# First weight of the second mixer split among the last feed-forward products, in the places of its later values and keys; those products in a fixed order, the second block's projections in other banks

## The chip, the cores and the metric

The kernel runs on one core of a Trainium2 chip. The metric is the device time of one execution in microseconds (us), taken as the median of several executions of the same program. The engines are named as the profile names them: PE is TensorE (PEld its weight loads), DVE is VectorE, ACT is ScalarE, POOL is GpSimd, SP issues the DMAs.

## The reference

A trunk of two layers over 256 tokens of width 1024, in float32. Each layer has a mixer and a feed-forward part, each behind a modulation and ahead of a norm:

```python
for layer in range(DEPTH):
    shift, scale, gate = ada_modulation(c, ada_w[layer, 0], ada_b[layer, 0])
    h = x * (1.0 + scale) + shift
    y = mixer_ab(h, ...) if layer % 2 == 0 else mixer_c(h, ...)
    x = layer_norm(DN_ALPHA * x + gate * y, ln_g[layer, 0], ln_b[layer, 0])
    shift, scale, gate = ada_modulation(c, ada_w[layer, 1], ada_b[layer, 1])
    h = x * (1.0 + scale) + shift
    y = squared_relu_mlp(h, mlp_w1[layer], mlp_w2[layer])
    x = layer_norm(DN_ALPHA * x + gate * y, ln_g[layer, 1], ln_b[layer, 1])
```

The change lies at the seam between the feed-forward part of layer 0 and `mixer_c` of layer 1, which begins with `q, k, v = split(h @ w_in)` and a rotation (rope) of `q` and `k`.

## The kernel before

**Precision by parts.** Every float32 product is made of three: each operand is split into a high part (a cast on ACT, `wh`) and a low part (the difference, a subtraction on DVE, `wl`), and `mm3` adds high by high, high by low and low by high into one PSUM bank. `split` (L170) does the two steps and returns the low one.

**Weights.** `plan` lists every 1 MB weight block in the order in which it is wanted. `fill` issues their DMAs on SP into four raw buffers (`NRAW`), and issues the next one when a raw buffer has been split. `take` splits the next block in two halves, ("w1", l, i) and ("w2", l, i) for the feed-forward part, ("ci", j) for the second mixer's input projection. Halves go to the pool `sp`, six places for high parts and six for low parts (`NSPLIT`); a place is free again when the last product that reads it is done. `need(key)` takes blocks up to a key, `ahead(n)` takes the next n.

**Order.** The program is written in one order, but a scheduler makes each engine's queue from it: of the instructions that it believes ready it takes the one with the lowest priority number. An instruction's number is its place in the program; `later(n)` shifts it by n (table `LATER`, default 200 for splits), and `behind(what, m)` forces m to stand behind a remembered instruction on the same engine without a wait. Each engine then runs its queue strictly in that order.

**The seam.** `mlp(0, ...)` works through 16 blocks i of the hidden width: `first(i)` makes the hidden values (96 products with 256 columns, then relu, square and split: `r`, `uh`, `ul`), `second(i, b, h)` adds them into the outputs for token block b (0 or 1) and half h of the width (6 products with 512 columns). For layer 0 (`held`) the products of i = 13 for b = 1 and all of i = 14 and 15 are left for `finish(b)`: 60 products, the last ones of the layer. `finish` also adds the residual (`residual`, L611 to L613, three DVE steps for each half). `renew` (L641) then does, for b = 0 and for b = 1: `finish(b)`, `norm(b)` (DVE L617 and L619, the power on POOL at L305, DVE L629), `modulate` (eight PE transposes at L446, the affine step L451 on ACT and L454 on DVE, then the split into `hTh` and `hTl`). Around the norm of b = 0 it takes ci 0 and ci 1.

**The projection.** `c_project(0, ...)` (L1058) calls `products(part, b)` in the order (0,0), (1,0), (0,1), (1,1), (2,0), (2,1); part 0 is q, 1 is k, 2 is v. Each is 24 products over two blocks: part 0 needs ci 0 and 1, part 1 needs ci 2 and 3, part 2 needs ci 4 and 5. Within one, products 1 to 6 read the first half of the first block, 7 to 12 its second half, and so on. Each has a bank of the pair `a` (`pa`, two banks), which is read by the rope (L474 to L478 on DVE) or copied (v). The pair `d` (`pd`) holds the feed-forward outputs of b = 1 until their residual, and later the attention's outputs. `vv` has two places of 1040 columns (values of the two head groups, L1064), `keys` is the place of the second group's key block (L1061).

Of the kernel before, what the change touches and what calls it, by code (L numbers as in the profile page):

```python
# [45 lines left out]
LATER = {("ci", 0, 0): -1000, ("ci", 0, 1): -1000, ("co", 1, 1): -300, ("wo", 2, 0): 400, ("ada", 1, 5): 500, "cM1": 30, "cO011": -300, "cO100": 100, "wO010": 30, "wO110": -40, "wY10": -80}  # L46

BEHIND = {("ci", 0, 0): "moments", ("ci", 1, 0): "norm", ("ci", 1, 1): "norm"}
# [18 lines left out]
def trunk(ctx: ExitStack, tc, c, x, pos, small, ln, ada, w_g, w_g1, w_uq, w_out, c_in, c_out, w1, w2, out):  # L67
# [52 lines left out]
    def mlp_plan(l, more, room):  # L120

        more, p = list(more), [("w1", l, 0)]
        for i in range(16):
# [15 lines left out]
              "w1": lambda l, i: w1[l, i], "w2": lambda l, i: w2[l, i]}  # L139
    raw, parts, state = {}, {}, {"next": 0, "taken": 0, "half": 0, "critical": None, "rows": None, "copied": None, "columns": None}  # L140
# [29 lines left out]
    def split(dh, dl, src):  # L170

        nc.scalar.copy(dh, src)  # L172
        return nc.vector.tensor_sub(dl, src, dh.bitcast(F32))  # L173

    def take():
# [10 lines left out]
        elif key[0] == "ada":  # L186
            j = state["half"]
            with later(LATER.get(key, ADA_LATER)):
                state["half"] = ada_product(key, j, w[:, j * D:(j + 1) * D])
            if state["half"]:  # L190
                return
        else:
            cuts = (0, 1024, 2048)
            parts[key] = []
            for part, (lo, hi) in enumerate(zip(cuts, cuts[1:])):
                if key in (("w1", 0, 0), ("w1", 1, 0), ("w2", 0, 15)):
                    wh, wl = (work.tile([P, 1024], F32R, name=n, tag="q4", bufs=5) for n in ("wh", "wl"))
                elif key in (("wo", 0), ("co", 0)):
                    if lo == 0:
                        wide = [t.rearrange("p k q -> p (k q)") for t in new_hT()]  # L200
                    wh, wl = wide[0][:, lo:hi], wide[1][:, lo:hi]
                else:
                    wh = sp.tile([P, 1024], F32R, name="wh", tag="wh")[:, :hi - lo]
                    wl = sp.tile([P, 1024], F32R, name="wl", tag="wl")[:, :hi - lo]
                half = (*key, part)
                with later(LATER.get(half, SPLITS_LATER)):
                    state["split"] = split(wh, wl, w[:, lo:hi])
                    behind(BEHIND.get(half), state["split"])
                parts[key].append((wh, wl))
# [27 lines left out]
    def mm3(ps, a, b, start, stop):  # L237

        nc.tensor.matmul(ps, a[0], b[0], start=start, stop=False)  # L239
        nc.tensor.matmul(ps, a[0], b[1], start=False, stop=False)  # L240
        nc.tensor.matmul(ps, a[1], b[0], start=False, stop=stop)  # L241
# [381 lines left out]
    def norm(b, zst, between=lambda: None):  # L623
        z, st = zst
        mv, rs = moments(st)
        between()
# [14 lines left out]
    def renew(finish, gb, i):  # L641
# [4 lines left out]
        for b in range(NB):  # L646
            finish(b, zs[b])
            if b == 0:
                norm(b, zs[b], lambda: ahead(1))
                behind("norm", state["split"])  # L650
                ahead(1)
            else:
                norm(b, zs[b])
# [312 lines left out]
    def mlp(l, hT, rest, rows):  # L966
# [5 lines left out]
        def first(i):  # L972
# [10 lines left out]
            nc.scalar.activation(r, ps, AF.Relu)  # L983
# [24 lines left out]
        def second(i, b, h):  # L1008
            halves = need(("w2", l, i))
            for f in range(2):  # L1010
# [3 lines left out]
                mm3(acc[b][h], (us[i][0][:, s], us[i][1][:, s]), (wh[:, o], wl[:, o]),  # L1014
                    i == 0 and f == 0, i == 15 and f == 1)
# [7 lines left out]
        for i in range(16):  # L1023
            if i >= 1:
                need(("w2", l, i - 1))
            if i > 1:
                first(i)
            if i == at:
# [12 lines left out]
        def finish(b, zst):  # L1041
            if held and b:
                for h in range(2):
                    second(13, b, h)
            for h in range(2):
                for i in (14, 15):
# [11 lines left out]
    def c_project(g, got):  # L1058
# [10 lines left out]
        def products(part, b):  # L1069
            ps = pa("ps_c")  # L1070
# [111 lines left out]
```

## Time and profile before

| | us |
|---|---|
| median of 3 runs | 666.57 |
| lowest and highest | 666.43, 667.81 |
| the profiled execution | 669.87 |
| its span, first to last instruction | 668.0 |
| PE busy in it | 633.9 (95%) |

All rows come from the one profiled execution; times in them count from the start of its span. A PE row's duration is modelled and overlaps the next, so the pace is read from the starts. A row's last bracket is the idle time of the engine ahead of it, and what ended it.

### The profile page before, as it was taken

How to read it: one execution, taken by the hardware profiler on the slowest of the kernel's cores; microseconds unless marked ns; L12 is line 12 of the kernel's file. 1: busy time of each engine (PE TensorE's matmuls, PEld its weight loads, DVE VectorE, ACT ScalarE, POOL GpSimd, SP SyncE). 2: the span in 40 equal slices, each digit the busy share in tenths (PEclk: the TensorE clock that was granted, in tenths of full speed). 3: DMA queues.
4: the chain of work that ended last, by engine and by line, in shares of the span. 5: the costliest groups of instructions: out<-in, count | busy, mean ns of one | idle time of the engine just before them, and what ended most of it. 6: DMA issues, size and time to landing. Idle time of an engine off the chain costs nothing. (4 is left out here: it accounts for less than half of the span.)

```text
span 668.0 us, 9850 instructions
## 1 busy us (share of the span) xinstructions
PE 633.9 (95%) x3802; PEld 530.5 (79%) x3802; DVE 471.5 (71%) x887; ACT 339.2 (51%) x538; POOL 37.5 (6%) x69
## 2 busy tenths in 40 slices
PE   6998898989999999999988999999999999999994
PEld 3555676868898989898865888888899989898983
DVE  2859996257779989986796996755867755554447
ACT  3324676345545454545534555773654555545440
POOL 5010010100000000200020000000000100000004
PEclk9999998989999999999998999999999999999998
DMA  8993889033779997999642586411467765565101
GB/s 300 409 414 145 301 325 358 12 126 127 289 275 323 351 378 274 354 353 382 234 151 101 167 354 225 137 65 63 149 230 253 282 223 189 199 236 192 67 1 63
DMA packets 24385, 151.52 MB, mean 227 GB/s; under 512 B 2833, under 2 KB 3089, under 8 KB 8338
## 3 DMA queue, kind: packets, MB, share of 16 engines
q1 hardware_dynamic: 24194, 150.71, 61.1%
q8 instruction: 30, 0.49, 0.3%
q10 hardware_dynamic: 144, 0.18, 0.1%
q14 instruction: 17, 0.14, 0.1%
HBM read 149.83 MB, written 1.05 MB: 226 GB/s over the span
## 5 line engine op out<-in xcount | busy, mean ns | idle before, releaser
L172 ACT CAST wh<-w_w 128x1024 fp32r<-128x1024 f32 x128 | 131.0, 1051 | 150.7 <-PE ps_m L240 67.2
L173 DVE TENSOR_TENSOR wl<-w_w,wh 128x1024 fp32r<-128x1024 f32 x128 | 153.4, 1222 | 67.8 <-ACT wh L172 67.6
L239 PE MATMUL ps_m<-hTh,wh 128*128 128x256 f32 x448 | 126.7, 283 | 0.0
L241 PE MATMUL ps_m<-hTh,wl 128*128 128x256 f32 x448 | 126.6, 283 | 0.0
L240 PE MATMUL ps_m<-hTl,wh 128*128 128x256 f32 x448 | 126.6, 283 | 0.0
L241 PE MATMUL ps_m<-wh,ul 128*128 128x512 f32 x256 | 101.3, 396 | 0.4 <-DVE ul L173 0.4
L239 PE MATMUL ps_m<-wh,uh 128*128 128x512 f32 x256 | 101.1, 397 | 0.0
L240 PE MATMUL ps_m<-wl,uh 128*128 128x512 f32 x256 | 100.8, 395 | 0.0
L325 DVE CUSTOM_DVE_ANT_0 junk<-w_ada,cB,sm 128x1024 bf16<-128x1024 f32 x68 | 87.2, 1282 | 17.0 <-DMA w_ada<-in_ada_dram 15.6
L240 PEld LDWEIGHTS ps_m<-hTl,wh 128*128 128x128 f32 x448 | 85.7, 191 | 1.3
L239 PEld LDWEIGHTS ps_m<-hTh,wh 128*128 128x128 f32 x448 | 85.6, 191 | 1.2
L241 PEld LDWEIGHTS ps_m<-hTh,wl 128*128 128x128 f32 x448 | 85.7, 191 | 0.0
L241 PEld LDWEIGHTS ps_m<-wh,ul 128*128 128x128 f32 x256 | 48.2, 188 | 12.0 <-DVE ul L173 1.0
L239 PEld LDWEIGHTS ps_m<-wh,uh 128*128 128x128 f32 x256 | 48.3, 189 | 10.2 <-ACT uh L172 0.6
L240 PEld LDWEIGHTS ps_m<-wl,uh 128*128 128x128 f32 x256 | 48.2, 188 | 9.7 <-DVE wl L173 0.2
L239 PE MATMUL ps_c<-wh,hTh 128*128 128x512 f32 x96 | 38.7, 406 | 4.8 <-DVE rope L476 3.3
L240 PE MATMUL ps_c<-wl,hTh 128*128 128x512 f32 x96 | 38.7, 405 | 0.0
L241 PE MATMUL ps_c<-wh,hTl 128*128 128x512 f32 x96 | 38.0, 396 | 0.0
L173 DVE TENSOR_TENSOR ul<-relu,uh 128x512 fp32r<-128x512 f32 (+1 forms) x36 | 22.6, 627 | 17.6 <-ACT uh L172 17.6
L542 ACT ACTIVATE prob<-prob,negm 128x128 f32<-128x128 f32 (+1 forms) x64 | 26.8, 452 | 14.6 <-DVE negm L538 14.5
L173 DVE TENSOR_TENSOR wl<-w_ci,wh 128x1024 fp32r<-128x1024 f32 x24 | 28.7, 1218 | 7.0 <-ACT wh L172 6.9
L172 ACT CAST wh<-w_ci 128x1024 fp32r<-128x1024 f32 x24 | 24.9, 1050 | 13.2 <-PE ps_c L241 7.0
(231 smaller groups left out, 994.0 us busy)
## 6 DMA issues: line engine op xcount, KB each, us to landing
w_w<-in_w_dram SPq DMA_DIRECT2D x64, 1024.0 KB, 5.0
w_ada<-in_ada_dram SPq DMA_DIRECT2D x40, 1024.0 KB, 7.1
w_ci<-in_c_in_dram SPq DMA_DIRECT2D x12, 1024.0 KB, 5.9
w_ada<-in_ada_dram SPq DMA_DIRECT2D x12, 512.0 KB, 9.5
w_wo<-in_w_out_dram SPq DMA_DIRECT2D x4, 1024.0 KB, 4.8
w_co<-in_c_out_dram SPq DMA_DIRECT2D x4, 1024.0 KB, 5.1
w_g<-in_w_g_dram SPq DMA_DIRECT2D x8, 356.0 KB, 9.1
early<-in_ada_dram SPq DMA_DIRECT2D x4, 512.0 KB, 8.7
```

The lines of the kernel that those rows point to most:

```text
L172: nc.scalar.copy(dh, src)
L173: return nc.vector.tensor_sub(dl, src, dh.bitcast(F32))
L239: nc.tensor.matmul(ps, a[0], b[0], start=start, stop=False)
L240: nc.tensor.matmul(ps, a[0], b[1], start=False, stop=False)
L241: nc.tensor.matmul(ps, a[1], b[0], start=False, stop=stop)
L325: state[key, j] = nc.vector.tensor_tensor_reduce(out=junk, in0=w, in1=cB, scale=1.0, scalar=bias, op0=ALU.mult, op1=ALU.add, accum_out=m)
L542: state["exp"] = nc.scalar.activation(pr[:, j, :nk], pr[:, j, :nk], AF.Exp, bias=negm[:, hd:hd + 1], scale=-1.0)
```

## The change

It does seven things at the seam.

1. The blocks w2 15, ci 0 and ci 1 are taken at the top of i = 15, ahead of `first(15)`. Before, w2 15 was taken after `first(15)`, and ci 0 and ci 1 in `renew`, around the norm of b = 0.
2. The splits of w2 15 get the early number -300. The relu of `first(15)` must stand behind the second cast of w2 15 on ACT (`"early"`). The four casts of ci 0 and ci 1 must stand behind the cast `uh` of block 15, their four low parts behind `ul` of block 15.
3. The first half of ci 0 is split into the two places of `vv`; the second half into one place of `sp` (high) and the place of `keys` (low). Before, ci 0 held two high and two low places of `sp`.
4. The last low part of ci 1 must stand behind `moments` of b = 0 (L619). In `renew`, ci 2 is taken after the norm of b = 0 and ci 3 after that of b = 1, their low parts behind the norm just made.
5. The 60 last products have a fixed order (`"last"`): all of i = 14 for b = 0, i = 15 half 0, i = 15 half 1; then for b = 1 i = 13, i = 14, i = 15 half 0, i = 15 half 1.
6. The products (0,1), (1,1) and (2,1) of the first head group take a bank of the pair `d`.
7. `norm` loses its argument `between`; `split` also remembers the cast, `mm3` returns its three products.

```diff
-LATER = {("ci", 0, 0): -1000, ("ci", 0, 1): -1000, ("co", 1, 1): -300, ...}
-BEHIND = {("ci", 0, 0): "moments", ("ci", 1, 0): "norm", ("ci", 1, 1): "norm"}
+LATER = {("ci", 0, 0): -1000, ("ci", 0, 1): -1000, ("w2", 0, 15, 0): -300, ("w2", 0, 15, 1): -300, ("co", 1, 1): -300, ...}
+BEHIND = {("ci", j, part): "norm" for j in (2, 3) for part in range(2)}
...
+                elif key == ("ci", 0):
+                    if lo == 0:
+                        wh, wl = (work.tile([P, 1040], F32R, name=n, tag="vv", bufs=2)[:, :1024] for n in ("wh", "wl"))
+                    else:
+                        wh = sp.tile([P, 1024], F32R, name="wh", tag="wh")
+                        wl = work.tile([P, 6, 256], F32R, name="wl", tag="keys").rearrange("p a k -> p (a k)")[:, :1024]
...
+                if half == ("w2", 0, 15, 1):
+                    state["early"] = state["cast"]
+                if key in (("ci", 0), ("ci", 1)):
+                    firsts.append((state["cast"], state["split"]))
...
         for b in range(NB):
             finish(b, zs[b])
+            norm(b, zs[b])
             if b == 0:
-                norm(b, zs[b], lambda: ahead(1))
-                behind("norm", state["split"])
-                ahead(1)
-            else:
-                norm(b, zs[b])
+                behind("moments", firsts[-1][1])
+            ahead(1)
             modulate(zs[b][0], b, i, hT)
...
-            nc.scalar.activation(r, ps, AF.Relu)
+            m = nc.scalar.activation(r, ps, AF.Relu)
+            if held and i == 15:
+                behind("early", m)
...
+                for m in mm3(acc[b][h], (us[i][0][:, s], us[i][1][:, s]), (wh[:, o], wl[:, o]),
+                             i == 0 and f == 0, i == 15 and f == 1):
+                    if held and (i > 13 or b and i == 13):
+                        behind("last", m)
+                        state["last"] = m
...
+            if held and i == 15:
+                need(("w2", l, i))
+                ahead(2)
             if i > 1:
                 first(i)
+            if held and i == 15:
+                for cast, low in firsts:
+                    behind("cast", cast)
+                    behind("vector", low)
...
+            if held:
+                for h in range(2):
+                    second(14, b, h)
             for h in range(2):
-                for i in (14, 15):
+                for i in (15,) if held else (14, 15):
                     second(i, b, h)
...
-            ps = pa("ps_c")
+            ps = (pd if g == 0 and b else pa)("ps_c")
```

## Rows read from the trace of the kernel before

**Rows 1.** The page's first part, busy time of PE in the whole span.

```profile
PE 633.9 (95%) x3802; PEld 530.5 (79%) x3802; DVE 471.5 (71%) x887; ACT 339.2 (51%) x538; POOL 37.5 (6%) x69
```

**Rows 2.** Busy time of each engine in stretches of the seam. Columns: stretch, its length, then busy us and instructions of PE, PEld, DVE, ACT and POOL, the granted clock of PE, DMA share, GB/s.

```profile
339.19:340.64 1.45, 0.00 (x1) 0.00 (x1) 1.45 (x3) 1.45 (x3) 0.00 (x0) 1.00 0.79 311
...
348.37:349.56 1.19, 0.38 (x2) 0.00 (x0) 1.19 (x2) 0.00 (x0) 0.85 (x1) 1.00 1.02 420
...
350.97:354.69 3.72, 0.40 (x2) 0.03 (x1) 3.69 (x10) 1.93 (x5) 0.00 (x0) 1.00 0.34 139
354.69:358.27 3.58, 3.58 (x10) 2.75 (x11) 0.58 (x1) 0.59 (x1) 0.00 (x0) 0.52 0.00 0
358.27:384.00 25.73, 25.73 (x121) 20.83 (x120) 22.35 (x33) 14.51 (x17) 0.00 (x0) 1.00 0.46 146
```

**Rows 3.** Waits from 340 to 360 us: who waited for whom, us in total, times, longest.

```profile
PEld ps_c L239 <- issue: 3.7, 1, 3.7
...
PE ps_c L239 <- DVE rope L476: 3.3, 1, 3.3
```

**Rows 4.** Groups of PE's instructions from 340.6 to 354 us (products of the projection). Columns: line, engine, operation, out<-in, shapes, count, then busy us and mean ns of one, then idle time ahead of them by what ended it.

```profile
L239 PE MATMUL ps_c<-wh,hTh 128*128 128x512 f32 x12 | 4.9, 407 | 1.4 <-ACT hTh L172 1.4
L240 PE MATMUL ps_c<-wl,hTh 128*128 128x512 f32 x12 | 4.8, 403 | 0.0
L241 PE MATMUL ps_c<-wh,hTl 128*128 128x512 f32 x12 | 4.8, 397 | 0.0
```

**Rows 5.** Timeline of PE, from the first of the 60 last products to the first products of the projection. Columns: start, us, engine, line, operation, out<-in, shapes, count, idle time ahead.

```profile
323.55 0.39 PE L239 MATMUL ps_m<-wh,uh 128*128 128x512 f32 x1
...
336.27 1.08 PE L446 MATMUL ps_mod<-ident,z 128*128 128x128 f32 x8 [0.42 <-DVE z L629]
...
338.57 0.39 PE L240 MATMUL ps_m<-wl,uh 128*128 128x512 f32 x1
338.80 0.39 PE L241 MATMUL ps_m<-wh,ul 128*128 128x512 f32 x1
340.64 0.50 PE L239 MATMUL ps_c<-wh,hTh 128*128 128x512 f32 x1 [1.45 <-ACT hTh L172]
```

**Rows 6.** Timeline of PE's weight loads around the second block's transposes and the wait behind them.

```profile
349.56 0.87 PEld L446 LDWEIGHTS ps_mod<-ident,z 128*128 128x128 f32 x8 [1.23 <-DVE z L629]
350.40 0.19 PEld L239 LDWEIGHTS ps_c<-wh,hTh 128*128 128x128 f32 x1
...
354.66 0.26 PEld L239 LDWEIGHTS ps_c<-wh,hTh 128*128 128x128 f32 x1 [3.73 <-issue]
```

**Rows 7.** Timeline of DVE from the splits of w2 15 to the first rope.

```profile
325.98 1.23 DVE L173 TENSOR_TENSOR wl<-w_w,wh 128x1024 fp32r<-128x1024 f32 x1 [2.82 <-ACT wh L172]
327.12 0.68 DVE L173 TENSOR_TENSOR ul<-relu,uh 128x512 fp32r<-128x512 f32 x1
...
329.86 1.29 DVE L611 TENSOR_TENSOR z<-ps_m,gateB 128x512 f32<-128x512 f32 x2 [0.92 <-PE ps_m L241]
...
333.83 0.15 DVE L619 TENSOR_SCALAR rs<-mv 128x1 f32<-128x1 f32 x1
333.91 1.23 DVE L173 TENSOR_TENSOR wl<-w_ci,wh 128x1024 fp32r<-128x1024 f32 x1
335.57 1.00 DVE L629 TENSOR_SCALAR z<-z,mv,rs 128x512 f32<-128x512 f32 x2 [0.44 <-POOL rs L305]
...
346.54 0.14 DVE L619 TENSOR_SCALAR rs<-mv 128x1 f32<-128x1 f32 x1
...
348.25 1.70 DVE L629 TENSOR_SCALAR z<-z,mv,rs 128x512 f32<-128x512 f32 x2 [0.44 <-POOL rs L305]
...
354.13 0.42 DVE L476 TENSOR_TENSOR rope<-ps_c,sinT 128x256 f32<-128x256 f32 x1
```

**Rows 8.** Groups of DVE's instructions from 336.4 to 348.2 us, between the two norms; columns as in rows 4.

```profile
L173 DVE TENSOR_TENSOR wl<-w_ci,wh 128x1024 fp32r<-128x1024 f32 x5 | 6.0, 1203 | 0.0
```

**Rows 9.** Timeline of ACT at the seam.

```profile
323.75 0.60 ACT L983 ACTIVATE relu<-ps_m 128x512 f32<-128x512 f32 x1 [4.71 <-PE ps_m L241]
...
325.85 0.62 ACT L172 CAST uh<-relu 128x512 fp32r<-128x512 f32 x1
...
331.48 2.00 ACT L172 CAST wh<-w_ci 128x1024 fp32r<-128x1024 f32 x2 [2.17 <-PE ps_m L241]
...
339.00 1.07 ACT L172 CAST wh<-w_ci 128x1024 fp32r<-128x1024 f32 x1
339.94 1.17 ACT L172 CAST hTh<-h 128x512 fp32r<-128x512 f32 x2
...
351.79 1.14 ACT L172 CAST hTh<-h 128x512 fp32r<-128x512 f32 x2
```

**Rows 10.** DMA issues from 308 to 314 us: the blocks w2 14 and w2 15, count, KB each, median us from issue to landing.

```profile
w_w<-in_w_dram SPq DMA_DIRECT2D x2, 1024.0 KB, 5.4
```

**Rows 11.** Timeline of SP: the same two issues (from the start of the first to the end of the second).

```profile
309.84 2.75 SPq L166 DMA_DIRECT2D w_w<-in_w_dram  x2
```

**Rows 12.** Timeline of POOL: a fill of a key block long before the seam, a power alone, and the power and the fill at the second norm.

```profile
125.77 0.95 POOL L1063 MEMSET ckT__3690<- 64x1024 f32 x1
...
141.95 0.56 POOL L305 TENSOR_TENSOR rs<-rs,mhalf 128x1 f32<-128x1 f32 x1 [14.28 <-DVE rs L619]
...
346.76 1.46 POOL L305 TENSOR_TENSOR rs<-rs,mhalf 128x1 f32<-128x1 f32 x1 [11.22 <-DVE rs L619]
348.28 0.95 POOL L1063 MEMSET ckT__3689<- 64x1024 f32 x1
```

More of the change, by code (lines that the diff above doesn't have):

```diff
@@ L45 @@
 SPLITS_LATER, ADA_LATER, ROWS_LATER = 200, 300, 0
-LATER = {("ci", 0, 0): -1000, ("ci", 0, 1): -1000, ("co", 1, 1): -300, ("wo", 2, 0): 400, ("ada", 1, 5): 500, "cM1": 30, "cO011": -300, "cO100": 100, "wO010": 30, "wO110": -40, "wY10": -80}
-BEHIND = {("ci", 0, 0): "moments", ("ci", 1, 0): "norm", ("ci", 1, 1): "norm"}
+LATER = {("ci", 0, 0): -1000, ("ci", 0, 1): -1000, ("w2", 0, 15, 0): -300, ("w2", 0, 15, 1): -300, ("co", 1, 1): -300, ("wo", 2, 0): 400, ("ada", 1, 5): 500, "cM1": 30, "cO011": -300, "cO100": 100, "wO010": 30, "wO110": -40, "wY10": -80}
+BEHIND = {("ci", j, part): "norm" for j in (2, 3) for part in range(2)}
 X_STEPS = ({8: 4, 9: 4}, 13), ({i: 1 for i in range(3, 11)}, 12)
@@ L139, in trunk @@
               "w1": lambda l, i: w1[l, i], "w2": lambda l, i: w2[l, i]}
+    firsts = []
     raw, parts, state = {}, {}, {"next": 0, "taken": 0, "half": 0, "critical": None, "rows": None, "copied": None, "columns": None}
@@ L170, in split @@
     def split(dh, dl, src):
-        nc.scalar.copy(dh, src)
+        state["cast"] = nc.scalar.copy(dh, src)
         return nc.vector.tensor_sub(dl, src, dh.bitcast(F32))
@@ L237, in mm3 @@
     def mm3(ps, a, b, start, stop):
-        nc.tensor.matmul(ps, a[0], b[0], start=start, stop=False)
-        nc.tensor.matmul(ps, a[0], b[1], start=False, stop=False)
-        nc.tensor.matmul(ps, a[1], b[0], start=False, stop=stop)
+        return [nc.tensor.matmul(ps, a[0], b[0], start=start, stop=False),
+                nc.tensor.matmul(ps, a[0], b[1], start=False, stop=False),
+                nc.tensor.matmul(ps, a[1], b[0], start=False, stop=stop)]
     crow = work.tile([1, 1040], F32, name="crow", tag="vv", bufs=2)[:, :D]
@@ L621, in moments, with norm @@
         return mv, rs
-    def norm(b, zst, between=lambda: None):
+    def norm(b, zst):
         z, st = zst
         mv, rs = moments(st)
-        between()
         for h in range(2):
@@ L1013, in second @@
                 o = slice(h * 512, (h + 1) * 512)
-                mm3(acc[b][h], (us[i][0][:, s], us[i][1][:, s]), (wh[:, o], wl[:, o]),
-                    i == 0 and f == 0, i == 15 and f == 1)
+                for m in mm3(acc[b][h], (us[i][0][:, s], us[i][1][:, s]), (wh[:, o], wl[:, o]),
[3 more added lines that the diff above has]
+                        state["last"] = m
         need(("w1", l, 1))
```

## The prediction

> **What bounds the kernel now.** I read the page's busy shares first: PE works 633.9 of 668.0 us [rows 1], so nothing but PE's idle time, and time at a low clock, can be won. The table of stretches then says where at this seam: PE stands still or nearly so in 339.19 to 340.64, 348.37 to 349.56 and 350.97 to 354.69, and in the 3.58 us behind the last of these it is busy at a mean granted clock of 0.52, that is mostly at the lower of its two levels, 1.2 GHz [rows 2]. Third, the waits and timelines name what each waited for. The pace of dense work is 0.23 us from one product of 512 columns to the next (338.57 to 338.80), and 0.105 us for a transpose (eight in 0.84 us, 349.56 to 350.40) [rows 5, 6]. Against that pace the seam loses:
>
> - before the first block's transposes, 0.42 us for the norm [rows 5];
> - before the first projection product, from 338.80 to 340.64, 1.84 - 0.23 = 1.61, for `hTh` [rows 5];
> - before the second block's transposes, 1.19 - 0.23 = 0.96, for the second norm [rows 2, 6];
> - before product block (0,1), 3.72 - 0.23 = 3.49 [rows 2]. The weight load is labelled "issue" with 3.7, but the product itself waits for DVE's L476 [rows 3], the last reader of (0,0)'s bank, which starts at 354.13 [rows 7];
> - at the low clock, 3.58 for six products and four transposes, worth 6 x 0.23 + 4 x 0.105 = 1.80, so 1.78 [rows 2].
>
> Together 8.26 us. That is the ceiling of the change, give or take half a microsecond of short waits.
>
> Why PE runs dry at 350.97 is in the groups: 3 x 12 = 36 projection products were done [rows 4], block (0,0) with 24 and half of (1,0) with 12. By the code the six places hold ci 0, 1 and 2; ci 3 needs a place of ci 0, which (0,1) must read first, and (0,1) needs a third bank where pair `a` has two. The input was there earlier: `hTh` of b = 1 is cast from 351.79, its first half being done some 0.6 later, at 352.4 [rows 9].
>
> **The change part by part.** *Banks.* (0,1) takes a bank of pair `d`, whose reader is the residual of b = 1, finished before the second norm at 348.25 [rows 7]. The wait for L476 goes. What is late next is `hTh` at 352.4: alone, the banks save 354.69 - 352.4 = 2.3 us, and PE's standstill shrinks to 1.4. Standstills of 1.2 and 1.45 left the clock at 1.00 in the next stretch, the one of 3.72 did not [rows 2], so I count the 1.78 too: 4.1 us.
>
> *Places.* ci 0 now holds one high and no low place of `sp`, so ci 1, ci 2 and the first half of ci 3 fit beside it (high 1 + 2 + 2 + 1, low 2 + 2 + 1). (1,0) can run 18 products ahead of (0,1) instead of 12: 6 x 0.23 = 1.4 us more cover. The last quarter needs a cast and a low part (1.07 + 1.23 [rows 7, 9]) while (0,1) has 12 products (2.8 us) left: hidden; uncovered it would cost 2.3.
>
> *Splits moved forward.* Between the two norms DVE makes five low parts of ci, 6.0 us [rows 8], in front of or within the chain that makes the second norm. With ci 0 done before the first norm, at most three are left there (ci 2, perhaps one of ci 1; ci 3 must follow the second norm). So the second norm comes 2 x 1.2 = 2.4 us earlier, and up to 3.6. Where do the moved ones go? ACT idles 4.71 ahead of the relu of block 15 and DVE 2.82 ahead of w2 15's first low part [rows 7, 9]. w2 15 is issued about 312.3 and lands 5.4 later, near 317.7 [rows 10, 11], so its two casts (2.0) fit before 323.75 and its low parts (2.4) into the 2.82. Then `uh`, now at 325.85 behind one of those casts, and `ul` come some 0.8 earlier, and ci 0's low parts fill 326.5 to 329, where DVE now works on w2 15 and waits 0.92 [rows 7]. The relu now waits for w2 15 on ACT; queued behind are `uh` and the casts of ci, and PE needs `uh` at 323.55 + 12 x 0.23 = 326.3. A landing 2 us late would still be covered.
>
> *Fixed order.* The 60 products take 13.8 us either way. Half 0 of b = 0 is complete after 18, near 327.9, half 1 after 24, near 329.3; now both residuals begin at 329.86 [rows 7]. DVE, with ci 0's low parts ahead, begins near 329.0 and needs the same 4.1 us for six steps and the moments. So the first norm moves by 0 to 1 us earlier, or 0.3 later if a low part of ci 1 gets in front; I take 0.6, the start of the residual moved from 329.86 less a little. A further low part still stands beside the power, as now (333.91). Behind the norm, the cast of ci at 339.00 now stands in front of `hTh` [rows 9]; the changed places let the casts of ci 1 and 2 go earlier, but their slots still come free with i = 13 and 14 of b = 1, near 332 and 335. I estimate that of the 2.03 us lost at the first norm and `hTh`, 1.0 is won (bounds -0.3 and 2.0).
>
> *Second norm.* With 1.0 from the start and 2.4 from the low parts, `hTh` of b = 1 is there between 349.0 and 350.0. PE starts the projection at 339.64 and has 42 products and eight transposes: 9.66 + 0.84 leads to 350.1. The standstill closes. So all of 0.96 + 3.49 + 1.78 = 6.23 goes; I leave 0.5 for imperfect order.
>
> *Key and value places.* The value blocks and the second key block can be filled only when ci 0 has been read, near 350. The fill of 0.95 that now runs at 125.77 [rows 12] then lands in a busy stretch of DVE. The price by rows: the second norm's pair took 1.70 where the first took 1.00 [rows 7], beside a fill of 0.95 [rows 12]: 0 if no such step is beside it, 0.7 if one is. It isn't needed until the second group's keys, four blocks of 24 products or 22 us on; I take 0, since few of DVE's steps there are of the norm's kind. The power shows the same kind of contact: 0.56 alone, 1.46 beside a low part [rows 12].
> The Trainium skill (SBUF — State Buffer, Who interferes with whom) speaks against this move: DVE and GpSimd share a port pair under an exclusive lock, held for a whole instruction, and the loser blocks entirely. By that rule the fill could cost its full 0.95, and the sum would give 661.5; the trace agrees in kind, with 0.70 for a fill of 0.95.
>
> *DVE behind the seam.* From 350.97 to 384.00 DVE is busy 3.69 + 0.58 + 22.35 = 26.6 of 33.0 us [rows 2]: 6.4 idle. PE's work there moves some 6 us forward. DVE's low parts and ropes must follow, and not every gap can be used. It was relieved of two low parts; I book 0.7 given back (bounds 0 and 4).
>
> **Sum.** 1.0 + 6.23 - 0.5 - 0.7 = 6.0 us. The profiled execution of 669.87 would become 663.9; it lies 3.3 above the median, so I take the difference off the median: 666.57 - 6.0 = **660.6**. After 384 PE is dense, so what is won at the seam should stay won.
>
> **The rivals.**
> *Banks alone.* The scheduler leaves low parts in front of the second norm, so `hTh` stays at 352.4. For it: those low parts have no idle time ahead of them [rows 8]. Against: two low parts are forced forward by the order. 4.1 saved: 662.4.
> *DVE takes it back.* The seam gains as above, but ropes and low parts fall behind by up to the 4 us of the bound above: 664.6. For it: 6.4 us of idle time against 6 needed. Against: eight steps of the new x in that stretch can wait.
> *The fill meets the chain.* The fill that moves to 350 stands beside a step of DVE on which PE waits, and costs the 0.70 of the second norm: 661.3. For it: DVE is busy then. Against: the wait must also reach PE.
> *It doesn't do what it says.* The first norm moves later and the ahead-of-need splits meet slots that come free no earlier; the bank's gain is eaten: 666 to 667.
> *Slower.* A standstill like the one at 350.97 comes back twice in the projection, because DVE's strict queue has a low part that waits for a place in front of a rope. Each costs 3.49 + 1.78 = 5.27, so two give 660.6 + 10.5 = 671. It decides from the second on: one alone leaves 665.9.
>
> **Chances.** Forecast, with its own range 658.5 to 662: 0.50; the fill 0.10; banks alone 0.16; DVE takes back 0.09; nothing 0.07; slower 0.08. Times within 0.2% (1.3 us) can't be told from no change by this measurement; so faster 0.85, same 0.07, slower 0.08. The range goes from the ceiling, 666.57 - 8.26 - 0.5 = 657.8, to just past the second rival, 664.8; it leaves out "nothing" and "slower".
>
> **What would show it.** Right: no wait of `ps_c` for L476; 42 products before (0,1), no granted clock under 1.00 near 350; two fewer low parts of ci between the norms; the second norm near 345; `uh` of block 15 near 325; (0,1) starting near 350. Wrong: PE waiting for `wl` of w2 15 or ci 3; the first norm later than 335.6; casts of ci in front of L451 on ACT; DVE without a gap and PE waiting for ropes from 350 to 376.

## The result and the profile after

| | before | after |
|---|---|---|
| median, us (4 runs each, on one chip) | 667.19 | 660.59 |
| lowest and highest | 666.43, 671.20 | 659.38, 662.98 |
| the profiled execution, and its span | 669.87, 668.0 | 662.98, 661.1 |
| first of the 60 last products to the first attention product (`ps_s`), in the trace | 59.57 | 53.33 |

The ratio is 0.9893, with a 95% interval of 0.9844 to 0.9942: faster, by 6.6 us, where 6.0 was forecast. In the traces 6.24 us of it lie between the first of the 60 last products (323.55 before, 323.29 after) and the first attention product (383.12 and 376.62). From there to the end both run nearly equally long, 284.84 and 284.49 us. Below, "the seam" is the stretch from the first of the 60 to that attention product.

The page's first part, of after, which answers to [rows 1]: span less PE's busy time is 661.1 - 631.9 = 29.2 us, where it was 34.1.

```profile
PE 631.9 (96%) x3802; PEld 530.6 (80%) x3802; DVE 470.5 (71%) x887; ACT 339.1 (51%) x538; POOL 34.4 (5%) x69
```

The stretches of the seam after, in the columns of [rows 2]:

```profile
323.29:335.36 12.07, 12.07 (x55) 9.82 (x54) 11.07 (x16) 8.18 (x10) 1.06 (x1) 1.00 0.78 297
337.79:340.28 2.49, 0.39 (x2) 0.00 (x0) 2.16 (x6) 2.41 (x6) 0.00 (x0) 1.00 0.49 204
340.28:346.19 5.91, 5.80 (x24) 4.42 (x25) 5.17 (x10) 0.00 (x0) 0.55 (x1) 1.00 0.19 43
346.19:349.60 3.41, 3.41 (x19) 2.94 (x20) 3.34 (x7) 2.68 (x6) 0.00 (x0) 1.00 0.56 238
349.60:352.40 2.80, 2.80 (x14) 2.29 (x13) 2.73 (x6) 0.06 (x1) 0.00 (x0) 1.00 0.00 0
352.40:376.62 24.22, 24.22 (x115) 19.54 (x113) 20.37 (x29) 14.43 (x17) 2.16 (x4) 1.00 0.49 169
```

Only one stretch is left in which PE stands still, 337.79 to 340.28; from there on PE is busy for all but 0.11 us, and the granted clock is 1.00 throughout, where the stretch behind the rope wait had 0.52 [rows 2]. The view of PE's waits from 323 to 377 us has one line; the rope's 3.3 [rows 3] and two waits for the norms are gone. The wait that is left, for the first `hTh`, has grown from 1.4 [rows 4] to 2.1:

```profile
PE ps_c L250 <- ACT hTh L173: 2.1, 1, 2.1
```

PE's timeline after, in the columns of [rows 5]:

```profile
336.22 1.03 PE L457 MATMUL ps_mod<-ident,z 128*128 128x128 f32 x8
337.01 0.48 PE L252 MATMUL ps_m<-wh,ul 128*128 128x512 f32 x1
337.32 0.39 PE L250 MATMUL ps_m<-wh,uh 128*128 128x512 f32 x1
337.55 0.40 PE L251 MATMUL ps_m<-wl,uh 128*128 128x512 f32 x1
337.79 0.39 PE L252 MATMUL ps_m<-wh,ul 128*128 128x512 f32 x1
340.28 0.51 PE L250 MATMUL ps_c<-wh,hTh 128*128 128x512 f32 x1 [2.10 <-ACT hTh L173]
...
346.19 1.11 PE L457 MATMUL ps_mod<-ident,z 128*128 128x128 f32 x8
...
351.26 0.40 PE L250 MATMUL ps_c<-wh,hTh 128*128 128x512 f32 x1
```

The first transposes no longer wait: 56 of the 60 products stand ahead of them and four behind, where it was 52 and eight. The same four products are then missing as cover for `hTh`, and the standstill ahead of the first projection product is longer than before, 2.49 us from start to start (337.79 to 340.28) where it was 1.84. The row at 351.26 is the first product of block (0,1), 42 projection products having run ahead of it; it waits for nothing.

DVE's timeline after, which answers to [rows 7]:

```profile
325.44 0.69 DVE L174 TENSOR_TENSOR ul<-relu,uh 128x512 fp32r<-128x512 f32 x1 [0.27 <-ACT uh L173]
326.39 2.36 DVE L174 TENSOR_TENSOR wl<-w_ci,wh 128x1024 fp32r<-128x1024 f32 x2 [0.26 <-ACT wh L173]
328.67 1.28 DVE L622 TENSOR_TENSOR z<-ps_m,gateB 128x512 f32<-128x512 f32 x2
...
332.26 1.21 DVE L174 TENSOR_TENSOR wl<-w_ci,wh 128x1024 fp32r<-128x1024 f32 x1
333.39 0.20 DVE L628 BATCH_NORM_AGGREGATE mv<-stats 128x2 f32<-128x12 f32 x1
333.63 0.15 DVE L630 TENSOR_SCALAR rs<-mv 128x1 f32<-128x1 f32 x1
333.70 1.22 DVE L174 TENSOR_TENSOR wl<-w_ci,wh 128x1024 fp32r<-128x1024 f32 x1
335.36 1.00 DVE L639 TENSOR_SCALAR z<-z,mv,rs 128x512 f32<-128x512 f32 x2 [0.44 <-POOL rs L316]
...
336.88 1.21 DVE L174 TENSOR_TENSOR wl<-w_ci,wh 128x1024 fp32r<-128x1024 f32 x1
338.01 0.72 DVE L465 TENSOR_SCALAR h<-ps_mod,facA,facB 128x128 f32<-128x128 f32 x2
...
345.59 1.00 DVE L639 TENSOR_SCALAR z<-z,mv,rs 128x512 f32<-128x512 f32 x2 [0.67 <-POOL rs L316]
```

The residual begins 1.19 us earlier (0.93 counted from the start of the seam), but the first norm does not: 12.07 us from that start, 12.02 before. A low part of ci 1 (332.26) stands between the residual's last step and the moments. The second norm comes 2.66 us earlier, at 345.59 [rows 7]. Between the two norms two low parts of ci are left, at 336.88 and 342.67, of five [rows 8].

ACT and POOL after, which answer to [rows 9] and [rows 12]:

```profile
324.79 0.62 ACT L173 CAST uh<-relu 128x512 fp32r<-128x512 f32 x1
...
336.86 2.21 ACT L462 ACTIVATE h<-ps_mod,facB,facA 128x128 f32<-128x128 f32 x6 [0.96 <-PE ps_mod L457]
339.09 1.14 ACT L173 CAST hTh<-h 128x512 fp32r<-128x512 f32 x2
...
348.42 1.24 ACT L173 CAST hTh<-h 128x512 fp32r<-128x512 f32 x2
```

```profile
334.26 1.06 POOL L316 TENSOR_TENSOR rs<-rs,mhalf 128x1 f32<-128x1 f32 x1 [53.80 <-DVE rs L630]
...
345.00 0.55 POOL L316 TENSOR_TENSOR rs<-rs,mhalf 128x1 f32<-128x1 f32 x1 [9.68 <-DVE rs L630]
...
353.14 0.95 POOL L1086 MEMSET ckT__3689<- 64x1024 f32 x1
354.48 0.95 POOL L1086 MEMSET ckT__3690<- 64x1024 f32 x1 [0.39 <-PE ps_c L251]
```

`hTh` of b = 1 is done 348.42 + 1.24 = 349.66, 1.6 us before (0,1) wants it at 351.26. The fills have moved behind the last read of ci 0, to 353 and 354. That of the second group's keys must, by the change's step 3; the other one, which stood beside the second norm at 348.28 [rows 12], stands behind the fills of `vv` in POOL's queue. With it gone the second norm's pair takes 1.00 us (345.59), where it took 1.70 [rows 7].

### The profile page after: what moved, and what is told of

It is laid out like the page before. It is cut to its first block, busy times and chain, and to the rows that moved or that the text cites. A ratio compares the mean times of both kernels' runs of the same rounds, so it can differ in the third digit from the quotient of the medians.

```text
span 661.1 us, 9849 instructions
## 1 busy us (share of the span) xinstructions
PE 631.9 (96%) x3802; PEld 530.6 (80%) x3802; DVE 470.5 (71%) x887; ACT 339.1 (51%) x538; POOL 34.4 (5%) x69
## 3 DMA queue, kind: packets, MB, share of 16 engines
HBM read 149.83 MB, written 1.05 MB: 228 GB/s over the span
```

## The experiments

Each kernel was timed beside the kernel before, in three groups, each on one chip. The medians of one and the same program lie up to 2.7 us apart between the groups (before: 666.54, 667.99, 669.19), so the seam's length, read from one trace of each, is the finer measure: in the thirteen traces the seam begins anywhere from 319.34 to 324.05 us, and what follows it takes 284.4 to 284.8. "Lost" is the seam less 50.28 us, which is what its 204 products and 32 transposes take at the pace (0.23 and 0.105 us [rows 5, 6]). "Clock" is the mean granted clock of the seam.

| kernel | median, runs | ratio to before, 95% | seam, us | lost, us | clock |
|---|---|---|---|---|---|
| before | | | 59.57 | 9.29 | 0.97 |
| the change (first result) | 660.59, 4 | 0.9893 [0.9844, 0.9942] | 53.33 | 3.05 | 1.00 |
| banks_alone | 664.31, 12 | 0.9944 [0.9913, 0.9974] | 55.69 | 5.41 | 1.00 |
| places_banks | 663.17, 8 | 0.9913 [0.9879, 0.9947] | 53.81 | 3.53 | 1.00 |
| no_banks | 663.79, 12 | 0.9950 [0.9924, 0.9976] | 56.51 | 6.23 | 0.97 |
| no_places | 662.21, 6 | 0.9902 [0.9866, 0.9938] | 54.50 | 4.22 | 0.97 |
| whole_change | 661.96, 8 | 0.9914 [0.9883, 0.9946] | 54.39 | 4.11 | 0.97 |
| free_order | 664.35, 12 | 0.9950 [0.9921, 0.9979] | 55.47 | 5.19 | 0.97 |
| low_parts_split | 662.73, 8 | 0.9910 [0.9876, 0.9943] | 52.35 | 2.07 | 1.00 |
| low_parts_behind | 660.57, 6 | 0.9889 [0.9851, 0.9928] | 52.51 | 2.23 | 1.00 |
| w2_unforced | 662.23, 7 | 0.9901 [0.9867, 0.9936] | 55.33 | 5.05 | 1.00 |
| low_part_behind_hTl | 659.61, 6 | 0.9867 [0.9824, 0.9909] | 52.40 | 2.12 | 1.00 |
| whole_change_again | 661.47, 6 | 0.9892 [0.9855, 0.9928] | 54.49 | 4.21 | 0.97 |

My theory was the sum of the prediction: most of the gain is the third bank and the low clock behind its wait, the rest comes from low parts that leave the two norm chains. The rival for the second half was that the banks alone do it, and that the rest of the change is idle.

**banks_alone.** The kernel before, with this line of the change only:

```diff
-            ps = pa("ps_c")
+            ps = (pd if g == 0 and b else pa)("ps_c")
```

> The kernel before with one edit: the projections of b = 1 in the first head group take banks of pair d. Theory (each part of the change takes its own share): the wait for the rope's L476 goes, (0,1) starts when hTh of b = 1 is cast, near 352.4, PE stands still 1.4 us instead of 3.7, the granted clock stays at 1.00: 2.3 + 1.8 = 4.1 us faster than before, ratio 0.994. Rival A (the banks are the whole change): 6.5 us faster, ratio 0.990. Rival B (the standstill is long enough for the low clock all the same): 2.3 us, ratio 0.9965.

The seam lost 59.57 - 55.69 = 3.88 us of its length, where 4.1 was priced. The product of (0,1) in its timeline:

```profile
350.07 0.50 PE L239 MATMUL ps_c<-wh,hTh 128*128 128x512 f32 x1 [1.10 <-ACT hTh L172]
```

The wait for L476 is gone, `hTh` is next with a standstill of 1.50 start to start (1.4 priced), and no low clock follows. So in the traces the bank is the larger half of the change, and not all of it. The medians allow 3.9 us, but they can't tell this kernel from the whole change: the intervals of the two ratios overlap.

**places_banks.** The same, and the places of ci 0 as in step 3 of the change:

```diff
+                elif key == ("ci", 0):
+                    if lo == 0:
+                        wh, wl = (work.tile([P, 1040], F32R, name=n, tag="vv", bufs=2)[:, :1024] for n in ("wh", "wl"))
+                    else:
+                        wh = sp.tile([P, 1024], F32R, name="wh", tag="wh")
+                        wl = work.tile([P, 6, 256], F32R, name="wl", tag="keys")...
```

> The kernel before with the banks of d and the places of ci 0, but with the splits taken and ordered as before. Theory: 42 products are ready ahead of (0,1) instead of 36, but the low part of ci 3 comes only behind the second norm, near 351.3, so PE works on from there: about 1.1 us more than the banks alone, 5.2 us faster than before, ratio 0.992; the second norm stays near 348. Rival A (banks are all): the same as the banks alone. Rival (the places matter most): as the whole change, 6.5.

The seam is 53.81 us: 1.88 less than with the banks alone, and only 0.48 more than with the whole change. (0,1) now has 42 products ahead of it and starts at 350.13, behind no standstill. The second norm starts where it did before (24.72 us from the start of the seam, 24.70 before). Six products more ahead of (0,1) are 1.4 us of cover; the other half a microsecond has another source. The fill no longer stands beside the second norm, whose pair took 1.70 us with the banks alone (first row) and takes 1.00 here (second row):

```profile
345.86 1.70 DVE L629 TENSOR_SCALAR z<-z,mv,rs 128x512 f32<-128x512 f32 x2 [0.44 <-POOL rs L305]
```

```profile
346.50 1.00 DVE L635 TENSOR_SCALAR z<-z,mv,rs 128x512 f32<-128x512 f32 x2 [0.44 <-POOL rs L311]
```

So the first half of `hTh` is cast by 28.17 us into the seam and not by 28.88 (the start of the casts and 0.62), and (0,1) starts at 28.35 and not at 28.93. The wait for the second transposes shrinks from 0.94 to 0.25 for the same reason.

The four steps that this kernel lacks (the order in which the splits are taken and forced, and that of the last products) together add the last 0.48 of the 6.24 us. Its median ratio, 0.9913, can't be told from those of the whole change, 0.9893, 0.9914 and 0.9892. Its standstill ahead of the first projection product is still 1.83 us, where the change's is 2.49, and two of the three traces of the change have a low clock behind that (below) and with it a longer seam, 54.39 and 54.49, than this kernel's.

**no_banks.** The change without its line on the banks:

```diff
-            ps = (pd if g == 0 and b else pa)("ps_c")
+            ps = pa("ps_c")
```

> The whole change without its banks: all projections in pair a. Theory: with the splits moved forward the rope of (0,0) is read by 351.6 in the changed kernel, while PE is busy with 42 products until about 351.1, so the bank comes free at almost the moment it is wanted: 0.3 to 1.0 us slower than the whole change, still 5.5 to 6.2 us faster than before, ratio 0.991. Rival A (the banks are the whole change): 4 us or more of the gain are lost, ratio 0.996 or above, and the low clock is back.

Its waits of PE in the seam:

```profile
PE ps_c L250 <- ACT hTh L173: 2.1, 1, 2.1
PE ps_c L250 <- DVE rope L487: 1.5, 2, 1.1
```

The rope waits are back, and two, as the rival "slower" had it; but one at a time they cost 0.56 and 1.23 us, not 3.49 each, and no low clock follows them. I had expected 0.3 to 1.0 for this kernel; the two waits alone are 1.8. Most of what is left of the 56.51 - 53.33 = 3.2 is a low clock further ahead, behind the standstill before the first projection product; against the two traces of the change that have one too, the seam is 2.0 to 2.1 longer.

**no_places.** The change without the six lines of places_banks, so that ci 0 goes to the pool `sp` as before (the diff there, taken back).

> The whole change, but ci 0 is split into pool sp as before. Theory: 36 products lead to about 349.8 and hTh of b = 1 is cast from 348.4 on, so (0,1) needs no more cover: 0 to 0.5 us slower than the whole change, ratio to before 0.990 to 0.991. Rival (the places make the gain, by cover and by early splits): 1.4 us or more slower than the whole change, ratio 0.992 or above, PE standing still ahead of (0,1).

54.50 us, but with a low clock in it that the first trace of the change did not have; against the two traces of the change that have one (54.39 and 54.49, below) it is 0.0 to 0.1 longer. (0,1) comes after 36 products, at 27.79 us, 0.3 behind the end of `hTh`. Without the low clock, about 1.1 us, it would meet `hTh` and wait for some of that; here too the fill is back beside the second norm, whose pair takes 1.71. So by this estimate the places are worth between 0 and 0.8 us once the splits are moved forward, and 1.88 where they are not: two remedies for one wait.

**whole_change and whole_change_again.** The changed kernel, without an edit, in the second and the third group, as measure of the kernels beside it.

> The changed kernel itself once more, beside the three below. It should give 0.989 of the kernel before, with an interval of about 0.4% to either side, and in its trace some 53.3 us from the first of the last 60 feed-forward products to the first attention product, the standstill of 2.5 us before the first value product in it again, since the order of the queues makes it. What is open is the low clock: behind the same standstill the trace of the changed kernel had none, and two of the experiments had a stretch of granted clock near 0.6. If it comes by chance from one execution to the next, this trace may have it, and is then some 1.7 us longer (55 us); if it hangs on the places and banks, it has none.

> The changed kernel beside the two others of this call, as their measure. It should lie 1.5 to 2.5 us above the kernel with the low part behind hTl and 0.5 to 1.5 us below the one with w2 15 unforced. In its trace the standstill of 2.49 us stands again before the first query product; of its two traces so far one had a low clock behind it (seam 54.39 us) and one had none (53.33 us), so either may come.

(In these texts and in those of low_parts_split and low_parts_behind, "value product" and "value weight" are slips: the first projection product is that of q, block (0,0), and the weight meant is ci 1, the second one of q.) Up to the first projection product both traces are the first one to within 0.02 us: norm at 12.06 and 12.07, that product at 16.99 and 16.99. Behind it both have the low clock. Of the latter, the standstill and what follows:

```profile
337.04:339.53 2.49, 0.39 (x2) 0.00 (x0) 2.16 (x6) 2.41 (x6) 0.00 (x0) 1.00 0.51 214
339.53:343.00 3.47, 3.46 (x9) 2.75 (x10) 3.47 (x5) 0.00 (x0) 0.00 (x0) 0.55 0.02 5
```

Nine products in 3.47 us at a mean granted clock of 0.55, that is mostly 1.2 GHz; in the first trace 15 ran in the 3.47 us behind the same standstill. Six products are 1.4 us; 0.26 of it comes back, since the second transposes then find their norm done. It costs 54.39 - 53.33 = 1.06 and 54.49 - 53.33 = 1.16 us, less than the 1.7 expected. The same program, with the same standstill, has it in one execution and not in another.

**free_order.** The change without the fixed order of the last products (step 5):

```diff
-                    if held and (i > 13 or b and i == 13):
-                        behind("last", m)
-                        state["last"] = m
+                    pass
```

> The changed kernel without the fixed order of the last feed-forward products (those of blocks 14 and 15, and of block 13 for the second half of the rows, may be put in any order that the planner finds). My theory: the fixed order is worth little by itself; it holds back work of the second half so that the first residual and norm come first. Without it the seam should be 0 to 1.5 us longer than the 53.3 us of the changed kernel, most of it as a later first norm (12.06 us from the start of the 60 products in the changed kernel). The rival is that the order is what keeps the second norm 2.7 us early: then the second norm falls back towards 348 and the seam to 55 or 56 us.

The first norm starts at 13.92 us instead of 12.06, the second at 23.57 instead of 22.30, the transposes wait 0.74 for the norm, and behind a standstill of 2.61 a low clock follows. Against the traces of the change that have one, the seam is 1.0 us longer; the loss lies ahead of the first projection product (18.03 against 16.99), as my theory had it. The second norm does fall back by 1.27, as the rival had it, but only half of the way to 24.70, and no more is lost behind the first projection product for it.

**w2_unforced.** The change without the early numbers of w2 15 and without the relu behind its second cast (step 2, first half):

```diff
-LATER = {..., ("w2", 0, 15, 0): -300, ("w2", 0, 15, 1): -300, ...}
+LATER = {...}
...
-            if held and i == 15:
-                behind("early", m)
```

> The changed kernel without the two orders that put the split of the last feed-forward weight (w2 15) ahead of the last hidden block: its early numbers and the relu that stands behind its second cast are taken out. Two of its four casts then stand around the last relu again, one of them between square and uh, and one of its low parts behind ul, in front of the low parts of ci 0. My theory: that forward move is what made room for ci 0 ahead of the first residual; one low part more there (1.2 us on VectorE) makes the first norm 1.0 to 1.3 us later (13.1 to 13.4 us after the start of the 60 products, 12.06 in the changed kernel) and the seam 54 to 54.6 us, or some 1.1 us more if a low clock comes behind the standstill. The rival: DVE has slack there, since the residual has to wait for the products anyway; then the norm stays at 12.1 and the seam at 53.3.

The timeline of DVE from the start of this seam (319.34):

```profile
321.77 1.23 DVE L174 TENSOR_TENSOR wl<-w_w,wh 128x1024 fp32r<-128x1024 f32 x1 [2.81 <-ACT wh L173]
322.92 0.68 DVE L174 TENSOR_TENSOR ul<-relu,uh 128x512 fp32r<-128x512 f32 x1
323.52 1.22 DVE L174 TENSOR_TENSOR wl<-w_w,wh 128x1024 fp32r<-128x1024 f32 x1
324.65 2.35 DVE L174 TENSOR_TENSOR wl<-w_ci,wh 128x1024 fp32r<-128x1024 f32 x2
326.93 0.68 DVE L622 TENSOR_TENSOR z<-ps_m,gateB 128x512 f32<-128x512 f32 x1
```

Two of w2 15's low parts stand where one was expected, one on either side of `ul`; the residual begins 7.59 us into the seam (5.38 in the change), the first norm at 14.26 instead of 12.06. The seam is 2.0 us longer, all of it without a low clock in either trace. The norm is 2.2 us later, and not 1.0 to 1.3, because two low parts stand ahead of the residual and not one. PE waits for the same two among the 60 products (0.6 in the view of waits, 1.9 with the short waits beside them). This runs beside DVE's delay and doesn't add to it: the transposes would have waited for the norm instead.

So without w2 15 forward, or without the fixed order, the change is 2.0 or 1.0 us worse; without both, and without the splits of ci 0 and ci 1 forward (places_banks), it is only 0.5 worse. Taking ci 0 and ci 1 forward puts low parts into DVE's queue ahead of the first norm, and by these runs the other two steps little more than pay for it. What each step would give by itself, on top of the banks and the places, was not run.

**low_parts_split.** The change, with the low parts of ci 1 and ci 2 held back further: the first one of ci 1 behind the moments, the second and those of ci 2 behind the first two modulating steps of DVE (`firsts` holds ci 2 as well here, and `modulate` remembers its last step on DVE as "hv20").

```diff
             if b == 0:
-                behind("moments", firsts[-1][1])
+                for _, low in firsts[2:3]:
+                    behind("moments", low)
             ahead(1)
             modulate(zs[b][0], b, i, hT)
+            if b == 0:
+                for _, low in firsts[3:]:
+                    behind("hv20", low)
```

> The changed kernel with one step more. In it the first norm came no earlier than before, because two low parts of the second value weight (1.2 us each on VectorE) stand ahead of the row moments and beside the power; so the transposed rows come late and TensorE stands for 2.5 us before the first value product. Here one of these low parts goes behind the moments, and the other, with the low parts of the next weight, behind the first modulating step of the first rows. If the two low parts set that standstill, the first norm comes 1.0 to 1.2 us earlier, the standstill shrinks from 2.5 to about 1.3 us, and the time falls by 1 us against the changed kernel (0.9875 of before), or by more where a low clock came behind the standstill. If instead ScalarE or the transposes set it, the norm comes earlier and the standstill stays: same time. If the postponed low parts now delay the second value weight for the first products, a wait on a low part shows at those, and the time is the same or up to 1 us longer.

The first norm comes at 11.08 us, 0.98 earlier, the first projection product at 14.91, 2.08 earlier. DVE's timeline shows why it is more than the norm's part:

```profile
335.13 1.01 DVE L639 TENSOR_SCALAR z<-z,mv,rs 128x512 f32<-128x512 f32 x2 [0.44 <-POOL rs L316]
337.38 0.73 DVE L465 TENSOR_SCALAR h<-ps_mod,facA,facB 128x128 f32<-128x128 f32 x2 [1.24 <-ACT h L462]
338.03 0.68 DVE L622 TENSOR_TENSOR z<-ps_m,gateB 128x512 f32<-128x512 f32 x1
338.62 1.22 DVE L174 TENSOR_TENSOR wl<-w_ci,wh 128x1024 fp32r<-128x1024 f32 x1
339.75 1.29 DVE L174 TENSOR_TENSOR hTl<-h,hTh 128x512 fp32r<-128x512 f32 x2
```

DVE idles ahead of its two modulating steps, where in the change a low part of ci 2 stands in front of them. With them in time, ACT's queue makes the first `hTh` behind its fifth `h` (338.27) and the first projection product starts as that ends, at 338.95; in the change both `hTh` stand behind all six and that product starts as the second ends (340.28). From norm to product it is 3.83 us instead of 4.93. Then a low part at 338.62 holds `hTl` back, and 0.74 is lost at the first product that reads `hTl` (340.49). The seam is 0.98 shorter, as expected of the time. The medians don't show it: 662.73 beside 661.96 for the change, 0.9910 and 0.9914.

**low_parts_behind.** As low_parts_split, but all four low parts of ci 1 and ci 2 stand behind the modulating steps:

```diff
             if b == 0:
-                for _, low in firsts[2:3]:
+                for _, low in []:
                     behind("moments", low)
...
             if b == 0:
-                for _, low in firsts[3:]:
+                for _, low in firsts[2:]:
                     behind("hv20", low)
```

> As the kernel with one low part behind the moments, but with all four low parts of the second and third weight behind the first modulating step of the first rows: none stands between the residual and the first norm, nor beside the power (which took 0.55 us alone and 1.06 to 1.46 us beside a low part). If the low parts set the standstill, the norm comes 1.5 to 1.8 us earlier than in the changed kernel and the standstill shrinks to under 1 us: 1.5 us less time than the changed kernel. The rival is that the four low parts (4 x 1.2 us) now stand ahead of the second rows' residual and norm, or of the first value products, and what is won before the first products is lost before the second rows: same time or up to 2 us longer than the changed kernel, with the second norm after 346.

The norm comes at 10.56, 1.5 earlier, as expected, but the seam, 52.51, is only 0.82 shorter than the change's and no shorter than that of low_parts_split: the transposes stand earlier in PE's queue and wait 0.39 for the norm all the same, a product waits 0.80 for the low part that came late, and the second norm is at 23.39 against 22.30. The rival's place was right, its price (0 or a loss) was not.

**low_part_behind_hTl.** As low_parts_split, with the later low parts behind `hTl` of b = 0, which `modulate` remembers as "hT20":

```diff
                 for _, low in firsts[3:]:
-                    behind("hv20", low)
+                    behind("hT20", low)
```

> As the kernel with one low part of ci 1 behind the moments, but the last low part of ci 1 and those of ci 2 stand behind the low half of the first rows (hTl of b = 0), not behind the modulating step: in that kernel a low part of ci 1 ran at 338.62 in front of hTl and the second query product waited 0.74 us for hTl. My theory: that wait goes, the first norm stays at 11.1, the first query product starts near 15 us, the seam is 51.6 to 51.9 us (53.33 in the changed kernel, 52.35 with the low part in front) and no standstill of over 0.6 us is left in it, so no low clock either; the time is 1.5 to 2.5 us below the changed kernel. The rival: the low part of ci 1 comes too late for products 19 to 24 of the first block, as where both were postponed (0.80 us lost at 19.56), and the seam stays at 52.3 to 52.6.

The wait for `hTl` shrinks from 0.74 to 0.34, and the seam is 52.40, not 51.6 to 51.9. What took it back is neither of the two things that I named. Its rows of ACT and PE at the second block:

```profile
346.82 1.24 ACT L173 CAST hTh<-h 128x512 fp32r<-128x512 f32 x2
```

```profile
347.20 0.39 PE L252 MATMUL ps_c<-wh,hTl 128*128 128x512 f32 x1
347.49 0.50 PE L250 MATMUL ps_c<-wh,hTh 128*128 128x512 f32 x1
```

The product at 347.49 is the first of (0,1). It starts as the first half of `hTh` of b = 1 is cast (346.82 + 0.62); in the change there were 1.6 us to spare. PE has caught up with the second norm, which three low parts now stand in front of (23.35 us into the seam against 22.30): its transposes wait 0.49 us, and a further gain at the first norm is lost at the second. In its median this is the fastest kernel of the study, 659.61 beside 661.47 for the change. But the intervals of the ratios, 0.9824 to 0.9909 and 0.9855 to 0.9928, overlap, so that only the traces (52.40 against 53.33, or 54.4 with a low clock) say that it is better.

## Why the prediction was right, and which terms were not

The time, 660.6 predicted and 660.59 measured, is closer than the terms are, and this closeness is luck: the gain was 6.6 us and not 6.0, the median of the kernel before was 667.19 beside the change and not 666.57, and the terms missed both ways. What held is that the gain lies behind the first projection product, in the waits there and in the low clock behind the rope wait. By its own steps:

- *The ceiling* of 8.26 us left out short waits, put at half a microsecond. The losses of the whole seam before sum to 9.29, so these were 1.0.
- *Banks*: priced at 4.1 alone, measured 3.88 (banks_alone). The standstill behind it was put at 1.4 and was 1.50 (1.27 over the pace). Right, and shown.
- *Places*: 1.4 us of cover, 42 products ahead of (0,1). The 42 are there; on top of the banks the step gave 1.88, half a microsecond of it by the fill that left the second norm.
- *Splits moved forward*: two, at most three, low parts fewer between the norms and the second norm 2.4 to 3.6 earlier; it was three fewer and 2.66. `uh` of block 15 was to come near 325 and came at 324.79. So it did what it was to do, but little hung on it: 1.6 us were to spare at (0,1), and places_banks, with the second norm where it was, has a seam only 0.48 longer.
- *First norm and `hTh`*: 1.0 of 2.03 us was booked, with bounds of -0.3 and 2.0. From the start of the seam to the first projection product it was 17.09 before and is 16.99: 0.1. This is the step that failed. The prediction had the start of the residual at 329.0 (it was 328.67) and then named the cause that did occur, "0.3 later if a low part of ci 1 gets in front", and did not choose it. One low part stands there (332.26), and another, of ci 2, in front of the modulating steps (336.88); low_parts_split, which moves both, gains 2.08 at that place, the whole of the upper bound.
- *Second norm, rope wait, low clock*: 6.23 less 0.5. From the first projection product to the first attention product it is 42.48 before and 36.34 after: 6.14, where 5.73 was booked. The size was nearly right, and the cause that the prediction put first was not needed for most of it: places_banks has 36.71 there, 5.77 less than before, without the earlier second norm.
- *DVE behind the seam*: 0.7 given back. PE is busy in all 24.22 us from 352.40, so it was 0.
- *Fills*: 0. No product waits in the stretch in which they run (353.14 to 355.43), and DVE is not in the chain there. The rule of the Trainium skill that was weighed (SBUF — State Buffer, Who interferes with whom) would have let a fill hold a step of DVE for its whole 0.95. The rows have 0.70: in the four traces with a fill beside the second norm (before, banks_alone, no_banks, no_places) its pair takes 1.70 or 1.71, in the other nine 1.00. What the prediction overlooked is the other side of the move: the fill left the second norm, which was worth half a microsecond in places_banks.

So 1.0 + 5.73 - 0.7 = 6.03 stood against 0.1 + 6.14 + 0 = 6.24 in the traces: the sum had 0.9 too much at the first norm, 0.4 too little behind it and gave 0.7 back that was not lost, and these nearly cancelled. This is the one trace of the change without a low clock behind its standstill; in the other two the seam is only 5.2 and 5.1 us shorter than before, and the forecast had no term for that. The span fell by a further 0.26 ahead of the seam and 0.35 behind it, of which the change makes nothing that the traces show. The rival "banks alone" is refuted by the traces, 53.33 to 54.49 against 55.69, though not by the medians; "slower" by the absence of rope waits; no_banks shows its mechanism, at 0.56 and 1.23 us where 5.27 each was priced.

## What to carry to other kernels

When a wait is removed, look at once for the second one behind it: here the third bank, the longer lead and the earlier norm all shorten the same standstill, and leaving the banks or the places out of the whole change cost less than adding them to the kernel before had gained. Run the simplest steps by themselves before you keep the rest: two of the seven gave 5.76 of the 6.24 us. In a strict queue a piece of work done ahead of need must be given a place behind the chain, not only in front of the point that needs it; the places of four low parts (behind the moments, behind the modulating steps) decided 2.1 us ahead of the first projection product here, of which 1.0 was left at the end of the seam. Where two chains meet a dense engine in turn, find how much each has to spare before you pay for making one of them earlier.

## What was not expected of the hardware

**A low clock that comes in one execution and not in the next.** In seven traces PE stood still for 2.47 to 2.61 us (start to start) ahead of the first projection product: the three of the change, no_banks, no_places, free_order and w2_unforced. In five of them a stretch at the lower level follows (the mean granted clock of the next 3.47 us is 0.53 to 0.68), at 1.06 to 1.16 us by the traces of the change; in the first one and in w2_unforced none does. In the six traces in which that standstill was 1.84 or less, none follows it. The prediction had taken a standstill of 1.45 of idle time (1.84 from start to start) as safe and one of 3.72 as not. Those of 2.47 to 2.61 between them went either way, and why is open. The range forecast for such a kernel should hold that 1.1 us.

**The power and the low part.** At the seam's norms the power on POOL takes 0.55 us with no low part beside it (ten times in the thirteen traces) and 1.05 to 1.46 with one (sixteen times). In all sixteen it ends 0.4 us behind the end of the low part: in the change the low part of 333.70 ends at 334.92 and the power at 335.32. In low_parts_behind:

```profile
343.97 1.21 DVE L174 TENSOR_TENSOR wl<-w_ci,wh 128x1024 fp32r<-128x1024 f32 x1
```

```profile
344.13 1.46 POOL L316 TENSOR_TENSOR rs<-rs,mhalf 128x1 f32<-128x1 f32 x1 [11.37 <-DVE rs L630]
```

The ends are 345.18 and 345.59. The low part is no longer for it (1.21). The Trainium skill (SBUF — State Buffer, Who interferes with whom) says that a VectorE instruction with two inputs in SBUF contends with a GpSimd instruction that reads SBUF, and that the later one blocks until the first is done; these rows agree. So a low part that is queued right behind the step that feeds the power (L630) costs the norm chain 0.5 to 0.9 us, though on DVE it fills idle time.
